# A hybrid encoder layer: the attention's softmax divided after the product with V, x added after the attention's share of the output product, and the state space model's complex tables by three real products

## The chip, the cores and the metric

One core of one Trainium2 chip runs the whole layer in one launch. The metric is the device time in microseconds (us) of that execution; smaller is better. Five engines work side by side, each with a queue of its own: TensorE (PE: products and transposes), VectorE (DVE), ScalarE (ACT), GpSimd (POOL) and SyncE (SP), which here issues all transfers.

## The reference

One layer, x of shape (1, 2048, 1024), float32, cut to what matters:

```python
h = rms_norm(x, norm1); z = h @ w_in                  # q (8 heads x 64) | k, v (2 heads x 64) | u (512)
q, k = rms_norm(q, q_gain), rms_norm(k, k_gain)       # over each head's 64
scores = q k^T / 8 - slope * dist                     # a band: own block of 128 and both neighbours
m = max(max(scores), sink); p = exp(scores - m)
denom = sum(p) + exp(sink - m)
att = (p / denom) @ v                                 # (2048, 512)
# state space model, 32 groups of 16 channels, 64 complex states, both directions:
#   x_t = a x_{t-1} + B u_t  (complex), y = sum of Re(C x) + d u;  then gelu and a gated product
ssm = gelu(y) @ w_glu, value * sigmoid(gate)          # (2048, 512)
x = x + concat([att, ssm]) @ w_out
h = rms_norm(x, norm2)
x = x + square(relu(h @ w_ff1)) @ w_ff2               # d_ff 4096
```

## The kernel before

The sequence is 16 tiles of 128 tokens. A product in full precision is three TensorE products of split operands (`mm3`, lines 87 to 89: high by high, low by high, high by low). The two products of the feed-forward part use a recursion of seven products in place of eight for a 2 by 2 block matrix (`PRODUCTS` 1 to 7), so their operands are sums and differences of blocks.

The stages, in order of time in the profile:

- 0 to 134 us: norm of x, and the u columns of W_in.
- 134 to 345 us: for each tile q, k and v (`qkv_part`, tiles pq and pk), then the norm of q and k over each head: squares on ScalarE, `L924` sums them to ten numbers per token, `L925` to `L932` make their inverse root with one step of Newton, and `L935`, `L939`, `L941` apply it. Beside it runs a side stream with the state space model, in 16 pairs of groups: `pair_in` and `pair_out` build tables by complex products (L564, 512 columns each; six on VectorE for each of the two), and scans (L672, L675) and products (pvu, py, pkd) follow.
- 345 to 690 us: attention, in 32 units (tile n, key head g), each with four query heads. `front(u)` makes scores, maximum and exponentials, `back(u - LEAD)` transposes the probabilities (ptp, copied by ScalarE into pT), multiplies by V (pv) and by the attention's rows of W_out (poa), and adds x (`L1100`). x is loaded here and the sum is stored to x1_dr. The rest of the side stream runs between, at a rate set by `SIDE_STEPS`.
- 690 to 907 us: the gated product (`run_glu`, four quarters) and `out_quarter`: for each tile `out_ssm` makes the state space model's share of W_out (pos_), adds it to x1 read back from x1_dr (two buffers, `L1199`, `L1211`) and stores it; `norm2` follows, with the inverse root on GpSimd (`L1237`), and for each pair of tiles the four sums of blocks on GpSimd (`L1249` to `L1252`). All seven operands of a pair go to hc_dr. The first 1024 tokens' operands are read back (`L1282`) and transposed (pth, `L1292`) as right operands hb.
- 907 to 1540 us: the first feed-forward product (f_al and others), the first 1024 tokens, then the second; 1553 to 2199 us: the second feed-forward product.

A scheduler sets each engine's order within what the program's dependences allow; each engine takes its own queue in order, and a waiting instruction holds up all that stands behind it on that engine. The division in `softmax` before, on the probabilities:

```python
DVE.tensor_tensor(den, den, es, op=ALU.add)
DVE.reciprocal(rc, den)
for h in range(GQ):
    if h < 2: DVE.tensor_scalar(p[:, h, 0:w], p[:, h, 0:w], rc[:, h:h + 1], None, op0=ALU.mult)
    else:     ACT.activation(out=p[:, h, 0:w], in_=p[:, h, 0:w], func=AF.Copy, scale=rc[:, h:h + 1])
```

Of the kernel before, what the change touches and what calls it, by code (L numbers as in the profile page):

```python
# [20 lines left out]
P = 128  # L21
# [24 lines left out]
LEAD = 3  # L46
# [5 lines left out]
SIDE_STEPS = 8 * 61.0 + 16.0  # L52
# [5 lines left out]
def hymba_kernel(ctx: ExitStack, tc: tile.TileContext, x, norm1, w_in, q_gain, k_gain, sink,  # L58
# [9 lines left out]

    ident = cst.tile([P, P], F32, name="ident")
    make_identity(nc, ident)  # L70
    mhalf = cst.tile([P, 16], F32, name="mhalf")
    nc.gpsimd.memset(mhalf, -0.5)

    ACT, DVE, POOL = nc.scalar, nc.vector, nc.gpsimd
    dist = cst.tile([P, 3 * P], F32, name="dist")
    nsink = cst.tile([P, NH], F32, name="nsink")
# [36 lines left out]
    v_all = att.tile([P, NT, NKV * HD], F32, name="v_all")  # L113

# [10 lines left out]
    pv_n = sc.tile([P, NG, C16], F32, name="pv_n")  # L125
    ta_c = sc.tile([P, NG, 8], F32, name="ta_c")
# [3 lines left out]
    rmag = sc.tile([P, NG], F32, name="rmag")  # L130
    dmask = sc.tile([P, GH], F32, name="dmask")
    dcol = sc.tile([64, NG // 2], F32, name="dcol")
# [267 lines left out]
    g1 = pw.tile([P, KD], F32, name="g1")  # L400
# [138 lines left out]
    f_tiles = [{nm: pm.tile([P, 2, 2, GH], F32, name=f"{nm}{j}") for nm in ("f_r", "f_i")} for j in range(2)]  # L539
    yr_t = pm.tile([P, 4 * NCH], F32, name="yr")  # L540
# [61 lines left out]

    def pair_in(i, h):
# [6 lines left out]
        sh = [P, 2, C16, GH]  # L610
        xr, xi = (four(a[:, gs], 2).to_broadcast(sh) for a in (bb_r, bb_i))
        yr, yn = (four(a[:, gs], 3).to_broadcast(sh) for a in (pv_r, pv_n))
        tmp = pm.tile([P, 512], F32, tag="tmp", name="tmp").rearrange("p (g s h) -> p g s h", g=2, s=C16)
        v = {}
        for j, (nm, x1, x2, op) in enumerate((("b_r", xr, xi, ADD), ("b_i", xi, xr, SUB))):
            t = pm.tile(sh, F32, tag=f"v{j}", name="v")
            dv(t, x1, yr, MUL)
            yield
            dv(tmp, x2, yn, MUL)
            yield  # L620
            dv(t, t, tmp, op)
            yield
# [7 lines left out]
            v[nm] = vt  # L630
        yield
# [48 lines left out]
    def ssm_unrotate(i):  # L680
        b = st[i]
        tcs, tsn = b["t_c"], b["t_s"]
        xr, xi = (pm.tile([P, 4 * NCH], F32, tag=nm, name=nm) for nm in ("x_r", "x_i"))
# [15 lines left out]
    def pair_out(i, h):  # L699
# [10 lines left out]
        sh = [P, 2, C16, GH]  # L710
        cr, cn = (four(a[:, gs], 2).to_broadcast(sh) for a in (c_r, c_n))
        er, ei = (four(a[:, gs], 3).to_broadcast(sh) for a in (pw_r, pw_i))
        tmp = pm.tile([P, 512], F32, tag="tmp", name="tmp").rearrange("p (g s h) -> p g s h", g=2, s=C16)
        for nm, x1, x2, op in (("q_r", cr, cn, ADD), ("q_n", cn, cr, SUB)):
            t = pm.tile(sh, F32, tag=nm, name=nm)
            dv(t, x1, er, MUL)
            yield
            dv(tmp, x2, ei, MUL)
            yield
            dv(t, t, tmp, op)  # L720
            b[nm] = t
            yield
# [9 lines left out]
        ks = pm.tile([64, GH + C16 * GH], F32, tag="ks", name="ks")  # L732
# [154 lines left out]
    with tc.tile_pool(name="p1", bufs=2) as p1:  # L887
# [16 lines left out]
        def qkv_part(t):  # L904
# [18 lines left out]
            t3 = p1.tile([P, 10], F32, tag="t3", name="t3")  # L923
# [4 lines left out]
            DVE.tensor_tensor(t3, rs, rs, op=ALU.mult)  # L928
            DVE.tensor_tensor(t3, t3, ms, op=ALU.mult)
# [652 lines left out]
```

## Time and profile before

| | |
|---|---|
| median of 3 runs | 2199.15 us (2194.41 to 2200.61) |
| the profiled execution | 2200.2 us, its span 2198.4 us |
| TensorE busy | 2077.8 us, 95% of the span |
| VectorE, ScalarE, GpSimd busy | 1479.6, 1016.0, 590.3 us |
| mean granted TensorE clock | 0.98 |

The profile's times are of one execution, and busy shares are means over stages with different limits. Ends of matmuls are modelled, so TensorE looks busy through waits that are shorter than a matmul's tail. A line of a group gives the engine's line and operation, what it writes and reads, its count, busy time in us, the mean of one in ns, and the engine's idle time just before with what ended it.

### The profile page before, as it was taken

The page shows a single profiled execution, that of the slowest core. Times are in us where ns is not written, and L with a number is a line of the kernel's source. Part 1 is how long each engine was busy: PE and PEld are TensorE (multiplying, and loading weights), DVE is VectorE, ACT ScalarE, POOL GpSimd, SP SyncE. Part 2 cuts the span into 40 slices and gives each one's busy share as a digit, 9 for nine tenths or more (in the row PEclk, how much of TensorE's full clock was granted, in tenths as well). Part 3 has the DMA queues.
Part 4 walks back from the last instruction along what each step waited for, and adds up shares of the span by engine and source line. Part 5 has one row for each costly group of instructions (what it writes and reads, how often), then busy time and mean ns, then how long its engine had stood idle before and what let it go on. Part 6 is the DMA issues. An engine that isn't in the chain of part 4 may idle for free.

```text
span 2198.4 us, 30479 instructions
## 1 busy us (share of the span) xinstructions
PE 2077.8 (95%) x10546; PEld 1706.7 (78%) x10546; DVE 1479.6 (67%) x2806; ACT 1016.0 (46%) x2061; POOL 590.3 (27%) x451
## 2 busy tenths in 40 slices
PE   7999998999999997799999999999599999999999
PEld 7888886777767786688888788888487778778787
DVE  7959887998856644655445655554677776776765
ACT  4433336767666422455555655555342332333231
POOL 2000000000012223322332133221553663564441
PEclk9999999999999999799999999999799999999999
DMA  8925544333245448644445644442763443443344
GB/s 252 292 82 159 157 125 142 108 100 117 96 125 160 163 153 279 224 149 152 153 158 176 203 156 146 146 151 99 255 212 101 129 128 98 134 130 114 112 135 162
DMA packets 284394, 337.06 MB, mean 153 GB/s; under 512 B 62928, under 2 KB 211408, under 8 KB 284240
## 3 DMA queue, kind: packets, MB, share of 16 engines
q1 hardware_dynamic: 284240, 335.12, 46.9%
q8 instruction: 83, 1.36, 0.3%
q14 instruction: 71, 0.58, 0.1%
HBM read 206.11 MB, written 128.94 MB: 152 GB/s over the span
## 4 chain that ended last, share of the span: by engine, by line
PE 67%; DVE 13%; DMA 7%; POOL 5%; issue 3%; ACT 3%; SPq 1%; DVEq 0%; POOLq 0%; ACTq 0%
PE f L87 6%; PE f L89 6%; PE f L88 6%; PE f_al L89 5%; PE f_al L87 5%; PE f_al L88 5%; PE f_ga L87 3%; PE f_ga L89 3%; PE f_ga L88 3%; POOL w2s L1470 2%; PE pv L1075 1%; POOL fs L1496 1%; PE ptp L1065 1%; DVE acc L1541 1%; PE f_be L89 1%
## 5 line engine op out<-in xcount | busy, mean ns | idle before, releaser
L1541 DVE TENSOR_TENSOR acc<-f,acc 128x512 f32<-128x512 f32 x448 | 304.8, 687 | 164.6 <-PE f L89 158.0
L87 PE MATMUL f<-w2s,fs 128*128 128x512 f32 x896 | 352.9, 394 | 31.0 <-DVE acc L1541 15.7
L89 PE MATMUL f<-w2s,fs 128*128 128x512 f32 x896 | 351.4, 392 | 3.7 <-POOL fs L1496 3.7
L88 PE MATMUL f<-w2s,fs 128*128 128x512 f32 x896 | 351.3, 392 | 0.0
L1495 ACT ACTIVATE fs<-fr 128x512 fp32r<-128x512 f32 x224 | 141.6, 633 | 366.1 <-PE f L89 350.5
L1496 POOL TENSOR_TENSOR fs<-fr,fs 128x512 fp32r<-128x512 f32 x128 | 185.2, 1449 | 297.0 <-ACT fs L1495 255.8
L87 PEld LDWEIGHTS f<-w2s,fs 128*128 128x128 f32 x896 | 169.4, 189 | 74.1 <-ACT fs L1495 27.0
L1339 POOL TENSOR_TENSOR w1s<-w1r,w1s 128x512 fp32r<-128x512 f32 x96 | 135.2, 1409 | 311.9 <-ACT w1s L1338 303.0
L87 PE MATMUL f_al<-hb,w1s 128*128 128x512 f32 x512 | 201.0, 393 | 1.0 <-ACT w1s L1338 1.0
L89 PE MATMUL f_al<-hb,w1s 128*128 128x512 f32 x512 | 200.6, 392 | 1.1 <-DVE w1s L1339 0.9
L89 PEld LDWEIGHTS f<-w2s,fs 128*128 128x128 f32 x896 | 169.7, 189 | 40.3 <-POOL fs L1496 4.5
L88 PE MATMUL f_al<-hb,w1s 128*128 128x512 f32 x512 | 200.4, 391 | 0.0
L88 PEld LDWEIGHTS f<-w2s,fs 128*128 128x128 f32 x896 | 169.8, 190 | 34.7
L818 POOL TENSOR_TENSOR wgl<-wgr,wgh 128x512 fp32r<-128x512 f32 x8 | 10.4, 1311 | 521.0 <-DMA wgr<-in_w_glu_dram 508.2
L1339 DVE TENSOR_TENSOR w1s<-w1c,w1s 128x512 fp32r<-128x512 f32 x96 | 68.3, 711 | 88.0 <-ACT w1s L1338 88.0
L89 PEld LDWEIGHTS f_al<-hb,w1s 128*128 128x128 f32 x512 | 96.5, 189 | 22.0 <-DVE w1s L1339 1.3
L87 PEld LDWEIGHTS f_al<-hb,w1s 128*128 128x128 f32 x512 | 96.5, 189 | 21.3 <-ACT w1s L1338 1.4
L88 PEld LDWEIGHTS f_al<-hb,w1s 128*128 128x128 f32 x512 | 96.6, 189 | 19.6
L1338 ACT ACTIVATE w1s<-w1c 128x512 fp32r<-128x512 f32 x128 | 80.6, 630 | 49.7 <-PE f_al L89 48.4
L88 PE MATMUL f_ga<-hb,w1s 128*128 128x512 f32 x256 | 99.9, 390 | 0.0
L87 PE MATMUL f_ga<-hb,w1s 128*128 128x512 f32 x256 | 99.8, 390 | 0.0
L89 PE MATMUL f_ga<-hb,w1s 128*128 128x512 f32 x256 | 99.7, 389 | 0.0
(548 smaller groups left out, 4956.9 us busy)
## 6 DMA issues: line engine op xcount, KB each, us to landing
fr<-f_dr SPq DMA_DIRECT2D x224, 256.0 KB
w1r<-in_w_ff_dram SPq DMA_DIRECT2D x64, 512.0 KB
f_dr<-fs SPq DMA_DIRECT2D x128, 256.0 KB
f_dr<-f SPq DMA_DIRECT2D x96, 256.0 KB
w2r<-in_w_ff_dram SPq DMA_DIRECT2D x32, 512.0 KB
hs<-hc_dr SPq DMA_DIRECT2D x56, 256.0 KB
xt<-in_x_dram SPq DMA_DIRECT2D x16, 512.0 KB
q_dr<-qd SPq DMA_DIRECT2D x16, 512.0 KB
```

The source lines that it names most:

```text
L87: nc.tensor.matmul(ps_ap, lhsT=lh, rhs=rh, start=first, stop=False, skip_group_check=onto)
L88: nc.tensor.matmul(ps_ap, lhsT=lh, rhs=rl, start=False, stop=False, skip_group_check=onto)
L89: nc.tensor.matmul(ps_ap, lhsT=ll, rhs=rh, start=False, stop=last, skip_group_check=onto)
L818: eng_lo.tensor_tensor(lo, raw, hi, op=ALU.subtract)
L1065: nc.tensor.transpose(pt[:, h, :], p[:, h, kt * P:(kt + 1) * P], ident)
L1075: nc.tensor.matmul(po[g * HD:(g + 1) * HD, :], lhsT=v_all[:, lo + kt, g * HD:(g + 1) * HD], rhs=pT.pop((n, g, kt)), start=kt == 0, stop=kt ...
L1338: ACT.activation(out=t[:, 0], in_=src, func=AF.Copy)
L1339: (DVE if m in (6, 7, 3) else POOL).tensor_tensor(t[:, 1], src, t[:, 0], op=SUB)
L1470: (DVE if m in (6, 7, 3) and fp else POOL).tensor_tensor(t[:, 1], src, t[:, 0], op=SUB)
L1495: ACT.activation(out=t[:, 0], in_=src, func=AF.Copy)
L1496: (DVE if m in (6, 7, 3) else POOL).tensor_tensor(t[:, 1], src, t[:, 0], op=SUB)
L1541: DVE.tensor_tensor(a[:, cs], po, a[:, cs], op=ADD)
```

## The change

It does six things.

1. The probabilities are no longer divided. The eight inverse sums of a tile are spread to 64 columns each (`spread`, ScalarE), transposed by TensorE into a PSUM bank of tag "tr" (`spread_t`), and multiply the product with V (`an`); that product is copied out of PSUM first.
2. x is not added in the attention: the attention's share of W_out goes to x1_dr in halves by way of a ScalarE copy (`xa`). Where x1 is read back, `load_xa` loads x too (one buffer, xx) and adds it, 1024 columns on VectorE.
3. The tables of `pair_in` and `pair_out` come from three real products in place of four (`three`): five VectorE operations of 512 columns in place of six, for `pair_in` a small sum too. Five sums of 512 columns are added to the setup.
4. The inverse root of the q and k norm is a power on GpSimd, and k is scaled once, not in two halves.
5. The second 1024 tokens' operands are transposed straight from SBUF between the out tiles, and FF1 takes that half first. Only the first half goes by way of hc_dr, read back later. Of the last pair, operands 1, 2, 6 and 5 are transposed ahead of FF1 and the others inside its first block.
6. `LEAD` is 2 in place of 3, tiles of few columns are padded, the square's unused output in `norm2` goes to PSUM (tag "mm", two buffers, which pos_ uses too), and the GpSimd subtractions of FF1's first block move to VectorE.

```diff
-LEAD = 3
+LEAD = 2
-SIDE_STEPS = 8 * 61.0 + 16.0
+SIDE_STEPS = 8 * 57.0 + 16.0
...
+    def three(names, tags, name, x1, x2, gs, y1, dif, total, both=None):
+        sh = [P, 2, C16, GH]
+        if both is None:
+            xs = pm.tile([P, 2, GH], F32, tag="xs", name="xs", bufs=2)
+            dv(xs, x1[:, gs], x2[:, gs], ADD)
+        else:
+            xs = both[:, gs]
...
+        dv(tmp, four(xs, 2).to_broadcast(sh), four(y1[:, gs], 3).to_broadcast(sh), MUL)
+        yield None, None
+        for nm, tag, x, y, op in ((names[0], tags[0], x2, dif, ADD), (names[1], tags[1], x1, total, SUB)):
+            t = pm.tile(sh, F32, tag=tag, name=name)
+            dv(t, four(x[:, gs], 2).to_broadcast(sh), four(y[:, gs], 3).to_broadcast(sh), MUL)
+            yield None, None
+            dv(t, tmp, t, op)
+            yield nm, t
...
             DVE.tensor_reduce(ms, sq, axis=AX.X, op=ALU.add)
-            DVE.tensor_scalar(ms, ms, 1.0 / HD, EPS, op0=ALU.mult, op1=ALU.add)
-            ACT.activation(out=rs, in_=ms, func=AF.Sqrt)
-            DVE.reciprocal(rs, rs)
...
-            DVE.tensor_tensor(rs, rs, t3, op=ALU.mult)
+            DVE.scalar_tensor_tensor(ms, ms, HD * EPS, hsc, op0=ALU.add, op1=ALU.mult)
+            POOL.tensor_tensor(rs, ms, mhalf[:, 0:10], op=ALU.pow)
...
+        def spread_t(n):
+            pr_ = ps.tile([P, GQ, P], F32, tag="tr", name="ptr")
             for h in range(GQ):
+                nc.tensor.transpose(pr_[:, h, :], rb_t[n][:, h].rearrange("p g d -> p (g d)"), ident)
+            rT_t[n] = pr_
...
-            ACT.activation(out=ah, in_=pa3, func=AF.Copy)
-            DVE.tensor_tensor(al, pa3, ah, op=ALU.subtract)
+            ACT.copy(an, po.rearrange("p (h t) -> p h t", h=GQ))
+            DVE.tensor_tensor(an, an, rT_t.pop(n), op=ALU.mult)
+            ACT.activation(out=ah, in_=an, func=AF.Copy)
+            DVE.tensor_tensor(al, an, ah, op=ALU.subtract)
...
-            DVE.tensor_tensor(xr[:, cs], po, xr[:, cs], op=ALU.add)
-            if half == 1:
-                nc.sync.dma_start(out=x1_dr[n * P:(n + 1) * P, :], in_=xr)
+            xa = pb.tile([P, 512], F32, tag="xa", name="xa", bufs=2)
+            ACT.copy(xa, po)
+            nc.sync.dma_start(out=x1_dr[n * P:(n + 1) * P, cs], in_=xa)
...
+    def load_xa(n, bufs):
+        t = load_x1(n, po_, "x1", bufs)
+        xt = po_.tile([P, D], F32, tag="xx", name="xx", bufs=1)
+        nc.sync.dma_start(out=xt, in_=x2d[n * P:(n + 1) * P, :])
+        DVE.tensor_tensor(t, t, xt, op=ALU.add)
+        return t
...
-    early = right_operands(0, [(m, i) for i in range(4) for m in PRODUCTS])
-    for n, _ in enumerate(out_quarter(3)):
-        if n > 0:
-            for _ in range(7):
-                next(early, None)
+    x1 = load_xa(NT // 2, 2)
+    pend = None
+    for n in range(NT // 2, NT):
+        nx = load_xa(n + 1, 2) if n + 1 < NT else None
+        out_ssm(n, x1)
+        if n == 11:
+            sb_stack.close()
+        nc.sync.dma_start(out=x1_dr[n * P:(n + 1) * P, :], in_=x1)
+        if pend is not None:
+            for m in PRODUCTS:
+                trans(m, (n - NT // 2) // 2 - 1, pend[m])
+        if n == NT - 1:
+            for j, m in enumerate((1, 2)):
+                trans(m, 3, h2_t[n - 1][:, j * 512:j * 512 + 512])
+        pend = norm2(n, x1)
+        x1 = nx
```

Three places show how the instructions stand. VectorE in the qkv stage, one tile's norm of q and k (msq and rsq are its sums and inverse roots, the lines of 512 columns between belong to the side stream); before:

```order
L924 TENSOR_REDUCE msq<-sq 128x10
L564 TENSOR_TENSOR tmp<-bb_r,pv_n 128x512
L925 TENSOR_SCALAR msq<-msq 128x10
L564 TENSOR_TENSOR v<-v,tmp 128x512
L927 RECIPROCAL rsq<-rsq 128x10
L564 TENSOR_TENSOR tmp<-c_n,pw_i 128x512
L928 TENSOR_TENSOR t_2805<-rsq 128x10
L929 TENSOR_TENSOR t_2805<-t_2805,msq 128x10
L931 TENSOR_TENSOR rsq<-rsq,hsc 128x10
L930 TENSOR_SCALAR t_2805<-t_2805 128x10
L932 TENSOR_TENSOR rsq<-rsq,t_2805 128x10
L935 TENSOR_TENSOR sq<-pq,rsq 128x512
```

and of the change:

```order
L942 TENSOR_REDUCE msq<-sq 128x10
L578 TENSOR_TENSOR b_i<-b_i,t_c 128x512
L943 SCALAR_TENSOR_TENSOR msq<-msq,hsc 128x10
L947 TENSOR_TENSOR sq<-pq,rsq 128x512
L950 TENSOR_TENSOR kd<-pk,rsq 128x256
L954 TENSOR_TENSOR qd<-sq,qd 128x8x64
```

Of the short operations L925 to L932 one is left (L943), and L947, which needs the power that GpSimd makes of L943's output, stands right behind it here. In six of the 16 tiles nothing stands between the two, in the other ten one instruction.

VectorE in the output product, tiles 12 and 13 (before x_9115 is tile 12, x_9117 tile 13; in the change x_8913 and x_8965; ss and h belong to `norm2`); before:

```order
L1211 TENSOR_TENSOR x_9115<-pos__9119,x_9115 128x512
L1211 TENSOR_TENSOR x_9115<-pos__9133,x_9115 128x512
L1235 TENSOR_TENSOR ss_9149<-ss_9149 128x1
L1236 TENSOR_SCALAR ss_9149<-ss_9149 128x1
L1238 SCALAR_TENSOR_TENSOR h_9148<-x_9115,ss_9149,g_7874 128x1024
L1211 TENSOR_TENSOR x_9117<-pos__9160,x_9117 128x512
L1211 TENSOR_TENSOR x_9117<-pos__9174,x_9117 128x512
```

and of the change:

```order
L1253 TENSOR_TENSOR x_8913<-pos__8970,x_8913 128x512
L1293 TENSOR_TENSOR t_8958<-h_8948 128x512
L1253 TENSOR_TENSOR x_8913<-pos__8984,x_8913 128x512
L1241 TENSOR_TENSOR x_8965<-x_8965,xx 128x1024
L1342 TENSOR_TENSOR hb<-pth,hb 128x4x128 x2
L1278 TENSOR_TENSOR ss_9049<-ss_9049 128x1
L1279 TENSOR_SCALAR ss_9049<-ss_9049 128x1
L1281 SCALAR_TENSOR_TENSOR h_9048<-x_8913,ss_9049,g_8711 128x1024
L1342 TENSOR_TENSOR hb<-pth,hb 128x4x128 x2
L1253 TENSOR_TENSOR x_8965<-pos__9063,x_8965 128x512
```

The sum of the next tile's x1 and x (L1241, x_8965) now stands between a tile's out sums and its norm. The load of x1 for the tile after that waits, by its two buffers, for the norm (h_9048) behind it.

TensorE at the end of the output product (pth<-ident,h and pth<-ident,t are the transposes from SBUF; h_9192 is tile 14's norm, h_9245 tile 15's, the t's sums of the last pair); before:

```order
L88 MATMUL pos__9407<-wsl,sth 128x512
L89 MATMUL pos__9407<-wsh,stl 128x512
L1292 MATMUL pth<-ident,hs 128x128 x72
L87 MATMUL f_al<-hb,w1s 128x512
```

and of the change:

```order
L93 MATMUL pos__9216<-wsl,sth 128x512
L94 MATMUL pos__9216<-wsh,stl 128x512
L1340 MATMUL pth<-ident,h_9192 128x128 x8
L1340 MATMUL pth<-ident,t_9256 128x128 x4
L1340 MATMUL pth<-ident,h_9245 128x128 x4
L92 MATMUL f_al<-hb,w1s 128x512
```

Where 72 transposes of operands read back stood ahead of FF1, 16 stand now, eight of which need the last tile's norm and GpSimd's sums of it.

## Rows read from the trace of the kernel before

In a row of a group: busy us, mean ns of one, then idle time just before it and what ended most of it.

**Rows 1.** Busy time by stretch (its first line names the columns).
```profile
core 0: us, PE busy (x) PEld busy (x) DVE busy (x) ACT busy (x) POOL busy (x), PEclk, DMA share, GB/s
134.00:345.00 211.00, 199.97 (x1348) 173.31 (x1346) 191.32 (x436) 71.45 (x198) 1.11 (x11) 0.99 0.45 136
345.00:384.00 39.00, 28.33 (x179) 21.93 (x179) 28.49 (x98) 30.63 (x82) 0.00 (x0) 0.91 0.56 162
384.00:630.00 246.00, 241.08 (x1539) 184.83 (x1538) 211.46 (x579) 173.13 (x462) 0.00 (x0) 1.00 0.33 104
...
850.00:907.00 57.00, 37.58 (x182) 28.80 (x181) 28.12 (x47) 21.56 (x43) 12.99 (x13) 0.80 0.90 298
```

**Rows 2.** Groups of VectorE by line, 134 to 345 us.
```profile
L939 DVE TENSOR_TENSOR kd<-pk,rsq 128x128 f32<-128x128 f32 x30 | 7.2, 279 | 0.0
...
L564 DVE TENSOR_TENSOR v<-bb_r,pv_r 128x512 f32<-128x512 f32 x10 | 6.8, 684 | 17.2 <-DMA u_dr<-ut 17.2
...
L927 DVE RECIPROCAL rsq<-rsq 128x10 f32<-128x10 f32 x15 | 3.1, 209 | 1.8 <-ACT rsq L926 1.8
...
L932 DVE TENSOR_TENSOR rsq<-rsq,t 128x10 f32<-128x10 f32 x15 | 2.5, 166 | 0.3
```

**Rows 3.** TensorE in order of time, 230 to 243 us (start, length, instruction).
```profile
234.91 1.05 PE L637 MATMUL pvu<-u,vt 128*128 128x128 f32 x8
...
239.28 0.40 PE L89 MATMUL pq<-wqh,hl 128*128 128x512 f32 x1
239.52 0.40 PE L87 MATMUL pq<-wqh,hh 128*128 128x512 f32 x1
```

**Rows 4.** Groups of VectorE by line, 345 to 690 us.
```profile
L1054 DVE TENSOR_SCALAR p<-p,rc 128x384 f32<-128x384 f32 (+1 forms) x64 | 24.0, 416 | 0.4
L1100 DVE TENSOR_TENSOR xr<-poa,xr 128x512 f32<-128x512 f32 x32 | 21.8, 687 | 5.7 <-PE poa L89 4.1 <-DMA xr<-in_x_dram 1.4
L1082 DVE TENSOR_TENSOR al<-pv,ah 128x512 fp32r<-128x512 f32 x16 | 10.9, 680 | 3.1 <-ACT ah L1081 3.1
```

**Rows 5.** Groups of ScalarE by line, 345 to 690 us.
```profile
L1067 ACT COPY pT<-ptp 128x512 f32<-128x512 f32 x92 | 50.8, 582 | 21.0 <-PE ptp L1065 20.7
L1056 ACT ACTIVATE p<-p,rc 128x384 f32<-128x384 f32 (+1 forms) x64 | 35.1, 596 | 8.2 <-DVE rc L1051 7.8 <-DVE ks L736 0.2
```

**Rows 6.** SyncE's queue in order of time, 774 to 800 us.
```profile
776.95 0.32 SPq L1261 DMA_DIRECT2D x_dr<-x  x1
...
781.06 0.39 SPq L1199 DMA_DIRECT2D x<-x_dr  x1
...
791.68 0.37 SPq L1199 DMA_DIRECT2D x<-x_dr  x1
```

**Rows 7.** VectorE in order of time, 864 to 912 us.
```profile
877.57 0.69 DVE L1211 TENSOR_TENSOR x<-pos__9393,x 128x512 f32<-128x512 f32 x1 [3.67 <-DMA x<-x_dr]
...
881.02 1.28 DVE L1238 SCALAR_TENSOR_TENSOR h<-x,ss,g 128x1024 f32<-128x1024 f32 x1 [0.73 <-POOL ss L1237]
...
908.77 1.77 DVE L1339 TENSOR_TENSOR w1s<-w1c,w1s 128x512 fp32r<-128x512 f32 x1
```

**Rows 8.** TensorE in order of time, 864 to 912 us.
```profile
872.62 0.40 PE L89 MATMUL pos__9407<-wsh,stl 128*128 128x512 f32 x1
879.71 1.94 PE L1292 MATMUL pth<-ident,hs 128*128 128x128 f32 x8 [6.69 <-DMA hs<-hc_dr]
...
906.99 0.79 PE L87 MATMUL f_al<-hb,w1s 128*128 128x512 f32 x1 [1.03 <-ACT w1s L1338]
```

**Rows 9.** SyncE's queue in order of time, 826 to 909 us.
```profile
871.07 0.94 SPq L1199 DMA_DIRECT2D x<-x_dr  x1
...
900.70 2.07 SPq L1322 DMA_DIRECT2D w1r<-in_w_ff_dram  x4
```

**Rows 10.** Groups of VectorE by line, 690 to 907 us.
```profile
L1238 DVE SCALAR_TENSOR_TENSOR h<-x,ss,g 128x1024 f32<-128x1024 f32 x16 | 20.5, 1284 | 12.8 <-POOL ss L1237 12.1 <-DMA x<-x_dr 0.7
```

**Rows 11.** GpSimd in order of time, 784 to 800 us.
```profile
785.82 1.29 POOL L1249 TENSOR_TENSOR t<-h 128x512 f32<-128x512 f32 x1 [1.40 <-DVE h L1238]
```

More of the change, by code (lines that the diff above doesn't have):

```diff
@@ L399, in hymba_kernel @@
     wql = pw.tile([P, KD, 768], F32R, name="wql")
-    g1 = pw.tile([P, KD], F32, name="g1")
+    g1 = small(pw, KD, name="g1")
     hstack = ExitStack()
@@ L709, in pair_out @@
             b[nm] = f
[L710 to L721, printed above, removed]
+        for nm, t in three(("q_r", "q_n"), ("q_r", "q_n"), "q", c_r, c_n, gs, pw_r, pw_d, pw_s, c_s):
+            if t is not None:
+                b[nm] = t
             yield
@@ L1137, in back @@
             n, g = divmod(u, 2)
+            if g == 1 and n < NT:
+                sums(n)
             if n < NT:
@@ L1140, in back @@
                     p_trans(n, g, kt)
+                    if g == 1 and kt == 0:
+                        spread(n)
                     yield 0.44
@@ L1245, in norm2 @@
         t4 = pn.tile([P, 512], F32, tag="t4", name="t4")
-        nc.sync.dma_start(out=hc_dr[n // 2, 1], in_=b11)
-        nc.sync.dma_start(out=hc_dr[n // 2, 2], in_=b21)
-        nc.sync.dma_start(out=hc_dr[n // 2, 3], in_=b22)
-        POOL.tensor_tensor(t3, b22, b12, op=SUB)
+        first = n < NT // 2
+        if first:
+            for m, t in ((1, b11), (2, b21), (3, b22)):
+                nc.sync.dma_start(out=hc_dr[n // 2, m], in_=t)
+        (POOL if first else DVE).tensor_tensor(t3, b22, b12, op=SUB)
         POOL.tensor_tensor(b12, b12, b11, op=SUB)
@@ L1408, in hymba_kernel @@
     load_w1(1)
+    left_w1(0, (1, 2))
+    for m in (1, 2):
+        split_w1(0, m)
     left_w1(0)
[L1410 removed]
+    for m in PRODUCTS[2:]:
         split_w1(0, m)
@@ L1415, in hymba_kernel @@
         blk = ff1_block(g)
-        switch = right_operands(1, [(m, i) for m in PRODUCTS for i in range(4)]) if g == NFB - 1 else None
+        switch = right_operands(0, [(m, i) for m in PRODUCTS for i in range(4)]) if g == NFB - 1 else None
         def after(m, g=g, switch=switch):
@@ L1425, in hymba_kernel @@
         next(blk)
+        if g == 0:
+            next(blk)
         if g + 1 < NG1:
@@ L1433, in hymba_kernel @@
             load_w1(g + 2)
-        for _ in range(5):
-            after(next(blk))
+        if g == 0:
+            after(2)
+            for m in PRODUCTS[2:6]:
+                trans(m, 3, pend[m])
+                after(next(blk))
+            trans(4, 3, pend[4])
+            pnb_stack.close()
+            ph_ = d1_stack.enter_context(tc.tile_pool(name="ph_", bufs=1))
+        else:
+            for _ in range(5):
+                after(next(blk))
         last = (blk, after)
```

169 lines of the change are left out of this document (89 added, 80 removed).

## The prediction

> **What bounds the kernel now.** I read the busy time by stretch first, then the groups of the busiest engine in each, then the order of time where TensorE stands still. TensorE is busy 95% of the whole, so a gain has to come from a stretch where something else sets its pace, and the change touches only what lies between 134 and 907 us. Of the rest, the two feed-forward products keep nearly all their code.
>
> 134 to 345 us is VectorE's: 191.3 of 211 us busy, and 17.2 of its idle time is a single wait at the start, for u [rows 1, 2]. After that it hardly stops. TensorE shows 200.0 us, but its ends are modelled: one matmul of 512 columns lasts 0.40 us in the rows and the next starts 0.24 us after it [rows 3]. Priced by distance, 16 tiles x 24 x 0.24 = 92 us for q, the same number at half the columns 46 us for k and v, and the remaining 580 of the 1348 matmuls at about 0.11 (eight of them in 1.05 us with one tail of 0.28) 64 us: some 200 us of work at most, 185 if the 0.24 is partly waiting. So TensorE stands right behind VectorE, with 11 to 26 us between.
>
> 345 to 384 us is the filling of the attention's pipeline: TensorE 28.3 of 39. From 384 to 630 us it is at 241.1 of 246 with VectorE at 211.5: here TensorE is the bound and VectorE follows [rows 1]. From 850 to 907 TensorE is busy 37.6 of 57 us and its granted clock is 0.80, while the transfers are at 0.90 [rows 1]. The last out product starts at 872.6, FF1 at 907.0: 34.4 us in which TensorE only transposes operands read back from DRAM and waits for them, once 6.7 us [rows 8].
>
> **The change, stretch by stretch.**
>
> *qkv, 134 to 345 us.* Removed per tile: seven short VectorE operations of 0.17 to 0.21 us, one added: net 6 x 0.17 = 1.0 us, 16 us in all; the k scaling, two of 0.28 us to one that I put at 0.45, 2 us [rows 2]. Of the 32 tables 18 fall in this stretch (10 and 8 of the two kinds, as the counts stand); each loses one operation of 0.68 us, less ten small sums at 0.2: 10 us. Together 28 us off VectorE. Added: L947 waits for GpSimd's power. Where a VectorE operation in `norm2` waits for such a power, it idles 0.73 us [rows 7]; in six tiles nothing covers that and in ten one instruction does, so 6 x 0.8 + 10 x 0.15 = 6 us. VectorE would save 22, and TensorE's own work allows 11 to 26, of which some stays waiting for hand-overs. I take -12, bounds -20 and -4. The five sums of the setup (3.4 us) fall in the 17.2 us wait for u; uncovered they would cost just that.
>
> *Attention, 345 to 690 us.* VectorE loses 24.0 (the division) and 21.8 (adding x), gains 16 multiplies at 0.68 = 11 us, loses about 14 x 0.68 = 10 us of tables and some 8 us of short operations whose number is halved: -53 of 274. ScalarE loses 64 x 0.596 = 38 us and gains 64 copies of 512 columns at 0.58 = 37: nothing [rows 4, 5]. But TensorE, the bound, gains 64 transposes at 0.11 us, +7, and saves no matmul. What it can get back is waiting: 10.7 us in the filling, 4.9 in the middle [rows 1], and what the modelled ends hide. One unit of `LEAD` less shortens the filling; I put 6 us there and 9 us for hand-overs that a freer VectorE makes sooner: -15 + 7 = -8. Bounds: -20 if all waits shown and the hidden ones go, +7 if none do. The new chain from spread over transpose, multiply and subtract lies two units behind the scores; a "tr" bank held for it would cost TensorE's next transposes up to 1 us a tile, and that is in the upper bound.
>
> *Output product, 690 to 907 us.* Removed: the gap of 34.4 us, of which the 72 transposes are 72 x 0.11 = 8 us of work that only moves, so 26 us of standing still. Three terms come back.
>
> First, the end. After the sum of x1 and x of tile 15, VectorE still has, in order, tile 14's norm, tile 15's out sums and tile 15's norm, then GpSimd two block sums. By the rows a norm takes 3.4 us from its last out sum to its end (two out sums of 0.69 from 877.57 end at about 878.9, the h behind them ends at 882.3), hence 3.5 + 0.7 x 5 (two out sums, three copies of operands) + 3.5, then 2 x 1.29 on GpSimd [rows 7, 11] and 1 us for transpose and copy: 14 us. TensorE's last out product runs into the first 3 of them and transposes fill about 1: +10.
>
> Second, the loop. x1 of tile n+1 may be loaded once the norm of tile n-1 is done, and that norm now stands behind the sum of x1 and x of tile n. One turn is: copies and norm 3.5 us, the load, the sum of x1 and x. The load: 871.07 to 877.57, 6.5 us, in a stretch of crowded transfers [rows 7, 9]; 781.06 was issued 4.1 us after the store of tile 0 that it waits for, so a quieter transfer takes about 4.1, and I take 4.6 [rows 6]. The sum: 1.28, as the norm's operation of 1024 columns with two operands from SBUF, which is the nearest row [rows 10]. In all 9.4 us, where TensorE needs 24 x 0.24 + 14 x 0.11 = 7.3. Four of the five turns from tile 10 to 15 are such loops, one is short: 4 x 9.4 + 5 = 43 against 37 us, +6.
>
> Third, the first eight tiles. There each fourth load of a quarter already stands in SyncE's queue behind the hc_dr stores that wait for GpSimd (781.06 the third, 791.68 the fourth [rows 6]), and xx and its sum now stand behind it: 2.5 us a quarter, 5, less about 3 for the third quarter, whose hc_dr stores are gone: +2.
>
> Sum: -26 + 10 + 6 + 2 = -8. Bounds: -22 if loads come in 4 us and the loop hides, +14 if every load takes 6.5.
>
> A rule that speaks against this: VectorE's subtraction at 908.77, two operands from SBUF while GpSimd ran one of its own, took 1.77 us where 0.69 is usual [rows 7]. The Trainium skill, SBUF - State Buffer, "Who interferes with whom", says that a VectorE instruction with two SBUF inputs contends with a GpSimd instruction that reads SBUF. By it the sums of x1 and x would stretch where they meet the block sums, and the whole would come some 5 us later than I forecast; no row shows such a sum yet.
>
> *FF1 and after.* Code as before but for the first block, where three operands of the last pair are transposed between products and their sums run on VectorE: +1, bounds -2 and +6.
>
> **Sum**: -12 - 8 - 8 + 1 = -27 against the profiled execution's 2200.2 us (1 us above the median): 2173.
>
> **The rivals.**
>
> *The loop in every tile (slower).* If the sum of x1 and x holds up VectorE's queue in both halves, with loads of 6.5 us and more under 1.5 MB a tile, ten tiles (two in each of the first two quarters, six in the second half) turn at 12 us in place of 7: +50, less 16 that the end still saves, +34; with -12, -8 and +1 the whole is +15, 2215. It decides from 3.5 us a tile on, that is a turn of 10.5 us. For it speaks the 3.67 us that VectorE waited for x at 877.57; against it that the 28 stores and 28 loads of operands that crowded the transfers there are gone. 0.14.
>
> *TensorE was the bound (no change).* VectorE's 75 us are freed where TensorE had little to gain: -4 in qkv, +7 in attention, -8 and +1: 2196. For it 241.1 of 246 us; against it the 11 to 26 us in qkv. 0.16.
>
> *Everything comes through.* -20, -18, -18, 0: 2144. For it, that VectorE's saving is three times what I book. 0.17.
>
> My forecast has 0.53.
>
> **How the numbers follow.** The range reaches from just above the full gain to the rival of no change: 2148 to 2202, which leaves out most of the slow rival and half of the full gain, about 0.2. A measurement tells 0.3% (6.6 us) from no change. Faster by more: 0.45 of my case, 0.17, and 0.06 of the no-change rival: 0.68. Within: 0.06 and 0.08, and 0.01 of the slow one: 0.15. Slower: 0.02, 0.02 and 0.13: 0.17.
>
> **What would show it.** Right: the qkv stretch about 12 us shorter, VectorE there below 170 us; in the attention VectorE near 220 us and TensorE's share unchanged; turns of the x1 sums of 9 to 10 us in tiles 12 to 15; FF1 starting near 879. Wrong: qkv as long as before with TensorE at 95% of it (TensorE was the bound); waits of TensorE for "tr" banks in the attention; sums of x1 and x of 2 us and more beside GpSimd; VectorE waiting over 5 us for x1 in each tile.

## The result and the profile after

The changed kernel takes 2234.72 us (median of 4 runs, 2229.36 to 2239.9) where the kernel before, run beside it, takes 2199.8: a ratio of 1.0164, 95% interval 1.0133 to 1.0195. It is slower by 35 us, where I had forecast 27 us less; the measured time lies outside the range of 2148 to 2202.

The profiled execution has a span of 2235.3 us. To place the 37 us I measure three stages in both traces by the starts of TensorE's products in order of time: qkv from the first pq to the last pk, attention from there to the last poa, output from there to the first f_al.

| stage | before | after | difference | forecast |
|---|---|---|---|---|
| qkv | 211.1 | 228.0 | +16.9 | -12 |
| attention | 335.6 | 366.4 | +30.8 | -8 |
| output | 226.6 | 214.9 | -11.7 | -8 |
| FF1 (f_al) | 630.3 | 631.3 | +1.0 | +1 |

Of the attention's 30.8 us 5.7 are moved work: 42 products of the gated part (pglu) stand in it after and 20 before, at 0.26 us each, and they are gone from the output stage. So without moved work the output stage is 6 us better and the attention 25 worse. After FF1 nothing differs by more than a microsecond.

Busy time by stretch of the changed kernel, the columns as in [rows 1]; 134 to 362 us is its qkv stage, and 402 to 680 us does what 384 to 630 us does there (some 100 scores, 75 copies of transposed probabilities):

```profile
134.00:362.00 228.00, 205.68 (x1366) 177.34 (x1365) 174.88 (x331) 68.71 (x187) 34.55 (x26) 0.98 0.44 126
...
402.00:680.00 278.00, 263.61 (x1625) 192.38 (x1626) 176.78 (x465) 175.12 (x451) 0.00 (x0) 0.99 0.23 73
...
887.00:943.00 56.00, 42.71 (x210) 34.26 (x207) 38.35 (x57) 19.39 (x43) 17.39 (x16) 0.89 0.43 149
```

VectorE is busy 174.9 us in a stage that grew to 228, against 191.3 of 211 [rows 1]; in the steady attention 176.8 of 278 against 211.5 of 246. VectorE has less to do, and the stages are longer with it. The engine that shrank is not the one that set the end.

In the qkv stage VectorE's groups by line show the new wait (busy time and mean ns of one, then the idle time before them and what ended it):

```profile
L947 DVE TENSOR_TENSOR sq<-pq,rsq 128x512 f32<-128x512 f32 x15 | 10.4, 692 | 29.2 <-POOL rsq L944 29.2
...
L950 DVE TENSOR_TENSOR kd<-pk,rsq 128x256 f32<-128x256 f32 x15 | 6.2, 414 | 0.0
```

and GpSimd's, in the same view of the same stage, what it waits for:

```profile
L944 POOL TENSOR_TENSOR rsq<-msq,mhalf 128x10 f32<-128x10 f32 x15 | 33.4, 2229 | 179.8 <-DVE msq L943 172.0 <-DVE xs L578 7.8
```

The power of ten columns takes GpSimd 2.23 us, and VectorE stands still for it 29.2 us in 15 tiles, 1.95 each. The wait from which I priced it, 0.73 us [rows 7], was for a power of one column, which takes 0.55 us (the kernel before):

```profile
880.43 0.55 POOL L1237 TENSOR_TENSOR ss<-ss,mhalf 128x1 f32<-128x1 f32 x1 [13.55 <-DVE ss L1236]
```

The merged k scaling takes 0.41 us, near the 0.45 I put.

So TensorE's waits in the stage (those that the profile shows, of all kinds) grew from 11.0 to 22.1 us; the largest single line, for whom, with us in total, times and the longest, is that for tt, a table that goes out to DRAM (ks) and comes back. Before and after:

```profile
PE py L759 <- DMA tt<-kd_dr: 4.5, 5, 2.4
```

```profile
PE py L777 <- DMA tt<-kd_dr: 7.4, 4, 3.2
```

In the attention TensorE's waits name the new chain; before, neither of these two lines was there:

```profile
PE poa L92 <- ACT ah L1110: 6.9, 7, 1.4
...
PE ptp L1090 <- DVE an L1109: 4.7, 5, 1.5
```

The product with W_out waits for ah, which now comes after a copy and a multiply; and the transposes of the probabilities wait for the multiply that frees the bank of tag "tr".

In the output stage the end is as forecast. In its last stretch above, 887 to 943, TensorE has 42.7 of 56 us at a granted clock of 0.89, against 37.6 of 57 at 0.80 in [rows 1]. TensorE in order of time, to compare with [rows 8]:

```profile
932.48 0.39 PE L94 MATMUL pos__9216<-wsh,stl 128*128 128x512 f32 x1
932.71 1.03 PE L1340 MATMUL pth<-ident,h 128*128 128x128 f32 x8
941.06 1.12 PE L1340 MATMUL pth<-ident,t 128*128 128x128 f32 x4 [7.32 <-POOL t L1295]
...
943.38 0.80 PE L92 MATMUL f_al<-hb,w1s 128*128 128x512 f32 x1 [0.35 <-ACT w1s L1400]
```

From the last out product to FF1 are 10.9 us in place of 34.4. The wait is for GpSimd's sum (t, L1295), as the order had it. The sums of x1 and x on VectorE, in order of time:

```profile
896.27 1.22 DVE L1241 TENSOR_TENSOR x<-x,xx 128x1024 f32<-128x1024 f32 x1
...
904.68 1.48 DVE L1241 TENSOR_TENSOR x<-x,xx 128x1024 f32<-128x1024 f32 x1 [1.75 <-issue]
...
915.31 1.22 DVE L1241 TENSOR_TENSOR x<-x,xx 128x1024 f32<-128x1024 f32 x1
...
922.83 1.49 DVE L1241 TENSOR_TENSOR x<-x,xx 128x1024 f32<-128x1024 f32 x1 [0.90 <-DMA x<-x_dr]
```

They turn in 8.4, 10.6 and 7.5 us, where I put 9.4. The load of x1 is issued right behind the norm, as the loop had it, and the sum follows a load of about 3.5 us in the first and the last of the three turns; in the second other instructions of VectorE, waits for ScalarE and the out sums among them, stand ahead of the sum when the load has had its 3.5 us, so that the load does not set that turn. SyncE's issue for the first turn (the norm's h ends at 901.13):

```profile
901.20 0.32 SPq L1233 DMA_DIRECT2D x<-x_dr  x1
```

One more row answers to the rule weighed in the prediction. Of the 16 sums of x1 and x five ran beside GpSimd's block sums. The other eleven took 1.21 to 1.23 us; four of the five took 1.48, 1.49, 2.14 and 2.33, the longest here with the two block sums beside it:

```profile
856.42 2.33 DVE L1241 TENSOR_TENSOR x<-x,xx 128x1024 f32<-128x1024 f32 x1
```

```profile
855.65 2.01 POOL L1295 TENSOR_TENSOR t<-h 128x512 f32<-128x512 f32 x1
857.74 2.15 POOL L1296 TENSOR_TENSOR t<-h,t 128x512 f32<-128x512 f32 x1
```

The fifth, at 785.72, took 1.22, and there the block sum took 2.20 in place of 1.29. That agrees with the Trainium skill, SBUF — State Buffer, "Who interferes with whom" (two operands from SBUF beside a GpSimd instruction that reads SBUF). The four together are 2.5 us longer, half of the 5 that the prediction weighed.

### The profile page after: what moved, and what is told of

Its sections match the earlier page's. It is cut to its first block, busy times and chain, and to the rows that moved or that the text cites. A ratio compares the mean times of both kernels' runs of the same rounds, so it can differ in the third digit from the quotient of the medians.

```text
span 2235.3 us, 30317 instructions
## 1 busy us (share of the span) xinstructions
PE 2098.6 (94%) x10610; PEld 1713.4 (77%) x10610; DVE 1444.0 (65%) x2579; ACT 1009.0 (45%) x2027; POOL 618.7 (28%) x459
## 4 chain that ended last, share of the span: by engine, by line
PE 44%; DVE 5%; POOL 3%; issue 2%; DMA 2%; ACT 0%; SPq 0%; DVEq 0%; POOLq 0%; ACTq 0%
PE f L92 6%; PE f L94 6%; PE f L93 6%; PE f_al L92 5%; PE f_al L94 5%; PE f_al L93 5%; PE f_ga L93 2%; PE f_ga L94 2%; PE f_ga L92 2%; POOL w2s L1546 2%; POOL fs L1572 1%; DVE acc L1617 1%; PE f_be L94 1%; PE f_be L93 1%; PE f_be L92 1%
## 5 line engine op out<-in xcount | busy, mean ns | idle before, releaser
L1401 POOL TENSOR_TENSOR w1s<-w1r,w1s 128x512 fp32r<-128x512 f32 x93 | 129.9, 1397 | 300.6 <-ACT w1s L1400 292.8
L1047 DVE CUSTOM_DVE_ANT_0 p<-pss,dist 128x384 f32<-128x384 f32 (+1 forms) x128 | 66.6, 537 | 65.8 <-PE pss L1046 62.0
L836 POOL TENSOR_TENSOR wgl<-wgr,wgh 128x512 fp32r<-128x512 f32 x8 | 10.6, 1341 | 330.6 <-DMA wgr<-in_w_glu_dram 321.5
L93 PE MATMUL f_ga<-hb,w1s 128*128 128x512 f32 x256 | 100.1, 391 | 1.4 <-DVE hb L1342 1.4
L92 PE MATMUL f_ga<-hb,w1s 128*128 128x512 f32 x256 | 99.9, 390 | 0.0
```

Source lines behind the costliest of these rows:

```text
L92: nc.tensor.matmul(ps_ap, lhsT=lh, rhs=rh, start=first, stop=False, skip_group_check=onto)
L93: nc.tensor.matmul(ps_ap, lhsT=lh, rhs=rl, start=False, stop=False, skip_group_check=onto)
L836: eng_lo.tensor_tensor(lo, raw, hi, op=ALU.subtract)
L1047: DVE.tensor_tensor_reduce(out=p_t[n, g][:, h, 0:w], in0=pss, in1=dist[:, off:off + w], scale=-SLOPE[g * GQ + h], scalar=-3.0e38, op0=ALU. ...
L1401: (DVE if m in (6, 7, 3) or g == 0 else POOL).tensor_tensor(t[:, 1], src, t[:, 0], op=SUB)
```

## The experiments

The theories: **A**, the GpSimd power and the division after the product each cost by themselves; **B**, both stages are longer because `LEAD` is 2 and the side stream is paced anew. Later ones are named where they come. Stage times are read as in the table above; ratios are to the kernel before on the same chip. A stage time is that of one profiled execution, which lies up to 7 us from its kernel's median (2201.8 against 2194.6 in "before, less VectorE"). Kernels with the same code in a stage show how far such times can be trusted: 225.8 to 228.0 us for qkv in the four with the power, 366.4 and 368.5, and 348.7 and 350.0, for the attention in two pairs. A difference of some 2 us is therefore read as none.

| kernel | median us | ratio (95%) | qkv | attention | output |
|---|---|---|---|---|---|
| changed | 2234.7 | 1.0164 (1.0133, 1.0195) | 228.0 | 366.4 | 214.9 |
| norm undone | 2228.8 | 1.0141 (1.0051, 1.0232) | 221.1 | 368.5 | 215.5 |
| division undone | 2215.1 | 1.0085 (1.0051, 1.0119) | 225.8 | 348.7 | 216.4 |
| both undone | 2207.3 | 1.0049 (1.0032, 1.0067) | 220.0 | 350.0 | 213.3 |
| both, py later | 2203.8 | 1.0043 (1.0027, 1.0060) | 213.6 | 349.0 | 212.9 |
| both and tables undone | 2203.8 | 1.0024 (1.0011, 1.0037) | 212.9 | 349.0 | 219.7 |
| and LEAD 3 | 2187.7 | 0.9954 (0.9936, 0.9972) | 214.7 | 338.3 | 214.1 |
| and x in the attention | 2187.4 | 0.9952 (0.9930, 0.9974) | 212.2 | 338.8 | 211.3 |
| and py later | 2193.2 | 0.9992 (0.9981, 1.0003) | 212.6 | 344.8 | 211.2 |
| tables undone, LEAD 3 | 2208.4 | 1.0056 (1.0030, 1.0081) | 222.3 | 346.2 | 212.5 |
| before, LEAD 2 | 2203.6 | 1.0024 (1.0008, 1.0041) | 212.0 | 341.6 | 227.4 |
| before, less VectorE | 2194.6 | 0.9987 (0.9976, 0.9998) | 210.0 | 337.2 | 228.7 |
| before, more VectorE | 2208.2 | 1.0039 (1.0022, 1.0056) | 212.5 | 343.4 | 225.8 |
| chain, no transposes | 2221.1 | 1.0128 (1.0093, 1.0162) | 226.0 | 358.9 | 209.1 |
| transposes, no chain | 2215.2 | 1.0089 (1.0054, 1.0124) | 227.4 | 348.8 | 215.1 |

**The norm's power undone**, to the changed kernel:

```diff
-            DVE.scalar_tensor_tensor(ms, ms, HD * EPS, hsc, op0=ALU.add, op1=ALU.mult)
-            POOL.tensor_tensor(rs, ms, mhalf[:, 0:10], op=ALU.pow)
+            DVE.tensor_scalar(ms, ms, 1.0 / HD, EPS, op0=ALU.mult, op1=ALU.add)
+            ACT.activation(out=rs, in_=ms, func=AF.Sqrt)
...
+            DVE.tensor_tensor(rs, rs, t3, op=ALU.mult)
```

> The changed kernel with the q and k norm's inverse root made as before (seven short VectorE operations and ScalarE's square root in place of the GpSimd power); all else as changed. Theory A (the power of ten columns takes GpSimd 2.2 us, VectorE stands still behind it 29 us in the qkv stage): the qkv stage, from its first pq to its last pk product, falls from 228 to 203 to 212 us, the attention stays at 360 to 370, the whole is 2209 to 2220. Theory B (both stages are longer because the side stream is paced differently and LEAD is 2): the qkv stage stays at 222 us or more, the whole within 6 us of 2235.

The qkv stage falls by 6.9 us to 221.1, between the two theories: the power costs, but of VectorE's 29 us of standing still only 7 reach the end of the stage, and 10 of the 17 us have another cause. With the division undone in both kernels the same step is 5.8 us (225.8 to 220.0). The attention doesn't move. The whole can't tell, since the kernel's two runs lie 14 us apart. In this kernel TensorE's largest wait of the stage has grown:

```profile
PE py L777 <- DMA tt<-kd_dr: 13.1, 5, 3.4
```

py, in TensorE's order, waits for the table, here longer than in either kernel above.

**The division undone**, to the changed kernel: each head's probabilities are multiplied by its inverse sum in `softmax`, and `pv` splits the product from PSUM.

```diff
-            ACT.copy(an, po.rearrange("p (h t) -> p h t", h=GQ))
-            DVE.tensor_tensor(an, an, rT_t.pop(n), op=ALU.mult)
-            ACT.activation(out=ah, in_=an, func=AF.Copy)
-            DVE.tensor_tensor(al, an, ah, op=ALU.subtract)
+            ACT.activation(out=ah, in_=pa3, func=AF.Copy)
+            DVE.tensor_tensor(al, pa3, ah, op=ALU.subtract)
```

> The changed kernel with the probabilities divided before they are transposed, as before (no spread, no ptr transposes, no multiply of the product with V); LEAD 2, the tables and x added later stay. Theory A (the transposes of the spread sums and the chain copy, multiply, split, subtract behind the product with V hold up TensorE): the attention, from the last pk to the last poa product, falls from 366 to 335 to 348 us, the whole is 2204 to 2218. Theory B (LEAD 2 and the pacing): the attention stays at 358 us or more.

The attention falls by 17.7 us to 348.7, the whole to 2215.1: near what theory A said, though VectorE is busier in the stage by 13 us (229.6 to 242.4) and ScalarE by 13 (239.3 to 251.9).

**Both undone.**

> Both of the above undone in the changed kernel: the tables by three products, x added later, the second half's operands from SBUF and LEAD 2 stay. Theory A: the two losses add, 2180 to 2197 us, under the kernel before. Theory B: over 2215.

2207.3: the two losses add, or nearly (by the medians 6.0 and 19.6 alone, 27.5 together; by the ratios 0.23%, 0.79% and 1.15%), but what is left is still slower than before, 0.49%, by 220.0 against 211.1 in qkv and 350.0 against 335.6 in the attention. Neither theory was enough. Theory **C** came from the wait for tt above: the tables by three products lengthen a round trip for which TensorE waits.

**LEAD 2 alone**, to the kernel before:

```diff
-LEAD = 3
+LEAD = 2
...
-                if h % 2 and u > 1 and wo_parts:
+                if h and u > 1 and wo_parts:
```

> The kernel before with LEAD 2 in place of 3 alone (and the split of W_out one call earlier, as the change has it, which LEAD 2 needs). Theory A: the attention is 330 to 342 us and the whole within 6 us of before. Theory B: the attention is 350 us or more, the whole 2212 or more.

6.0 us in the attention, of which eight more pglu products are 2, and +0.24% in the whole: a cost, where I had booked a gain of 6 us for a shorter filling. The filling is shorter: the first poa product starts 35.3 us after the last pk product, where it was 39.3. But what follows is 10 us longer, and TensorE's waits that the profile shows don't tell why (16.3 us in the stage, 20.2 before). It is far from the whole of theory B.

**The tables undone too**, to the kernel with both undone: `three` is out, `pair_in` and `pair_out` are as before.

> As the kernel with norm and division undone, and the tables by four products again (six VectorE operations of 512 columns for two tables in place of five, the side stream's rate as before). Theory C: in the qkv stage TensorE waits for the round trip of kd through DRAM (ks stored, tt loaded), which fewer steps between a table and its product no longer cover; then the qkv stage falls from 220 to 209 to 214 us, the attention from 350 to 337 to 345, the whole is 2186 to 2198. Theory D (the padded tiles, the merged k scaling or the x1 copies are what holds both stages): the qkv stage stays at 217 us or more.

The qkv stage falls by 7.1 us to 212.9, the attention stays at 349.0. So theory C holds for qkv and fails for the attention, and theory D, which has the stage at 217 us or more, is out. The whole gains 3.5 us by the medians and 0.25% by the ratios, whose intervals overlap, since the output stage gives 6.4 back (11 pglu products, 2.9 us of it, moved from the attention); the rest of that I can't place. The power stays in both the changed kernel and "tables undone, LEAD 3", and there the tables make 5.7 us in qkv (228.0 to 222.3).

**The later product**, which tests the round trip by itself: tables by three products stay, and py of a group's first pair is issued after the next group's first table.

```diff
-            yield from pair_y(i, 0)
             if i + 1 < NB4:
                 yield from pair_in(i + 1, 0)
+            yield from pair_y(i, 0)
             yield from pair_out(i, 1)
```

> The kernel with norm and division undone (tables by three products, LEAD 2), and in the side stream the product py of a group's first pair is issued after the next group's first table instead of before it, eight steps more between the store of ks and the product that needs tt. Theory C (TensorE waits in its order for the round trip of kd, 11.7 us in six waits, and loses its clock behind the long ones): those waits fall below 5 us, the qkv stage from 220 to 209 to 215 us, the whole to 2194 to 2203. Theory F (the table's own order is what slows the stage, not the trip): the qkv stage stays at 217 us or more.

TensorE's waits for tt in the two kernels, without and with the move:

```profile
PE py L777 <- DMA tt<-kd_dr: 11.7, 6, 2.7
```

```profile
PE py L777 <- DMA tt<-kd_dr: 2.6, 2, 2.0
```

The waits for tt fall from 11.7 to 2.6 us and the stage from 220.0 to 213.6, as theory C said and theory F did not: where py stands in TensorE's order matters. The whole can't confirm it: 6.4 us are 0.3%, the ratio falls by 0.06%, and each interval is 0.17% to either side. Nor is it the waits' length alone. With the move another wait comes in, for VectorE's table ahead of its transposes:

```profile
PE ptv L652 <- DVE v L578: 6.0, 4, 2.3
```

In all TensorE's waits in the stage fall by only 3 us (14.2 to 11.3). The rest of the 6.4 us is near what the clock gives back: the stage's mean granted clock, in the column before the last two, is 0.97 without the move and 0.99 with it, which over 214 us is some 4 us of full clock (an estimate from these figures).

```profile
134.00:354.00 220.00, 205.75 (x1365) 178.78 (x1363) 184.77 (x422) 73.61 (x203) 1.11 (x11) 0.97 0.45 130
```

```profile
134.00:348.00 214.00, 202.23 (x1364) 174.50 (x1362) 182.06 (x420) 73.94 (x205) 1.11 (x11) 0.99 0.47 134
```

In the stretch after the longest of the waits for tt, without and with the move:

```profile
174.00:182.00 8.00, 7.38 (x35) 6.93 (x36) 6.18 (x16) 1.10 (x2) 0.00 (x0) 0.58 0.13 46
```

```profile
174.00:182.00 8.00, 6.72 (x55) 6.31 (x55) 8.00 (x21) 2.36 (x6) 0.00 (x0) 1.00 0.60 172
```

TensorE ran 35 matmuls at a mean granted clock of 0.58 there (mostly the lower level, 1.2 GHz), where with the wait gone it ran 55, not all of them the same ones, at 1.00.

**LEAD 3, and x added in the attention again**, each on top of the one before:

> The same with LEAD 3: what is left of the change is x added later, the k scaling in one, the padded tiles and the second half's operands from SBUF. If LEAD 2 costs what it did alone (6 us in the attention), the attention is 331 to 339 us, the output stage 211 to 217 and the whole 2180 to 2191, faster than before. If LEAD 2 costs nothing here, the whole is within 3 us of the kernel above.

> The same with x added in the attention as before, so that of the change little but the second half's operands from SBUF is left. If the sum of x1 and x costs in the output stage what the loop in the prediction says (6 to 10 us) and the ScalarE copies bring nothing to the attention, the output stage is 203 to 210 us and the whole 2174 to 2186. If taking the sum off VectorE pays in the attention, the attention is 4 us longer or more than in the kernel above and the whole is not faster.

LEAD 3 takes 10.7 us off the attention (9 without seven pglu products that move), as expected if LEAD 2 costs, and both kernels are faster than the one before: 2187.7 and 2187.4, ratios of 0.9954 and 0.9952, with intervals clear of 1. Where x is added makes no difference in the whole: taking 32 sums of 512 columns off VectorE in the attention is worth nothing there that could be told (338.3 against 338.8), and the loop in the output stage costs 2.8 us, 4 without the five pglu products that move, less than the 6 to 10 expected. What is left of the change in the faster one, the second half's operands from SBUF, takes 15.3 us off the output stage (211.3 against 226.6). The padded tiles, the one k scaling and the side stream's x_r and x_i, which now lie in other tiles' buffers, a change that the list of six leaves out, stay in this kernel too, and its qkv stage is near the kernel before's (212.2 against 211.1).

**The move on top of that:**

> The same move in the kernel that keeps of the change the second half's operands from SBUF, the k scaling and the padding, with tables by four products, LEAD 3 and x added in the attention. TensorE's waits for tt are 8 us or less there already, so Theory C gives 2 to 6 us in the qkv stage (206 to 211 us) and 2180 to 2187 for the whole; if VectorE is the bound of that stage instead, nothing (within 2 us of 2187).

Nothing in qkv (212.2 to 212.6), and 6 us lost in the attention: a miss. The waits for tt fell here too, from 5.3 to 1.7 us, but a wait for the table (ptv, 5.9 us) took their place as above, and the stage's clock, 0.99 without the move already, had nothing to give back. In the attention's first 40 us TensorE's clock is lower with the move (0.74 against 0.87), and one wait of 6.5 us for ScalarE's copy stands in it:

```profile
PE ptq L1024 <- ACT pT L1094: 6.5, 1, 6.5
```

**The division at LEAD 3**, the changed kernel with the tables undone:

```diff
-LEAD = 2
+LEAD = 3
...
-            xa = pb.tile([P, 512], F32, tag="xa", name="xa", bufs=2)
+            xa = pb.tile([P, 512], F32, tag="xa", name="xa", bufs=1)
```

> The changed kernel with the tables by four products and LEAD 3 (one buffer for xa in place of two, for space): the division after the product and the GpSimd power stay. Theory A (the chain behind the product with V and the transposes cost by themselves): the attention is 350 us or more, the whole 2206 to 2222. Theory E (they cost only since LEAD 2 leaves no slack): the attention is 342 us or less.

346.2 us, between theory A and theory E: against 338.3 with the division on the probabilities it costs 7.9 us here, against 17.7 at LEAD 2. So part of its price seems to be the slack that LEAD 2 took away; the two pairs differ in the tables, the norm and xa's buffers too, so that this is not shown alone.

**Which half of the division costs.** Both kernels leave the division itself out. In the first the product is multiplied by a constant tile and nothing is transposed; in the second copy and multiply are gone and the bank is read by one column only:

```diff
-                if kt == hi - lo - 1:
-                    spread_t(n)
...
-            DVE.tensor_tensor(an, an, rT_t.pop(n), op=ALU.mult)
+            DVE.tensor_tensor(an, an, woh.bitcast(F32)[:, :, 0:P], op=ALU.mult)
```

```diff
-            ACT.copy(an, po.rearrange("p (h t) -> p h t", h=GQ))
-            DVE.tensor_tensor(an, an, rT_t.pop(n), op=ALU.mult)
-            ACT.activation(out=ah, in_=an, func=AF.Copy)
+            DVE.tensor_scalar(nm_t[n][:, 0:1], rT_t.pop(n)[:, 0, 0:1], 1.0, None, op0=ALU.mult)
+            ACT.activation(out=ah, in_=pa3, func=AF.Copy)
```

> The changed kernel without the transposes of the spread sums: the product with V is multiplied by a constant tile from SBUF instead (the sums' copy on ScalarE stays; the division itself is left out). If TensorE's 64 transposes and the tr bank that they hold are the loss, the attention falls from 366 to 347 to 353 us, the whole to 2214 to 2222. If the chain copy, multiply, split, subtract behind the product with V is, it stays at 358 us or more.

> The changed kernel with the transposes kept (one column of each bank is read, which frees it) and the product with V split straight from PSUM as before, without copy and multiply (the division is left out). If the chain is the loss, the attention falls to 350 to 357 us; if the transposes and the bank are, it stays at 360 us or more.

Without copy and multiply the attention is 348.8 us, where the division undone had 348.7, with the 64 transposes still there; of the 17.6 us that it falls, eight pglu products that move are 2. Without the transposes it is 358.9, and TensorE's wait behind the chain is the larger for it:

```profile
PE poa L92 <- ACT ah L1108: 15.3, 8, 3.2
```

So it is the chain. The transposes cost 7.5 us beside it, and some 2 without it (nine pglu products fewer stand in the 348.8 us than in the 348.7). That this is because the bank is held until the chain's multiply has read it fits the 4.7 us of ptp behind an above, but no run shows it alone.

**VectorE's share of the bound in qkv**, which the prediction began with: the kernel before without the step of Newton, and with two of them.

```diff
             DVE.tensor_tensor(t3, rs, rs, op=ALU.mult)
             DVE.tensor_tensor(t3, t3, ms, op=ALU.mult)
             DVE.tensor_scalar(t3, t3, -0.5, 1.5, op0=ALU.mult, op1=ALU.add)
+            DVE.tensor_tensor(rs, rs, t3, op=ALU.mult)
+            DVE.tensor_tensor(t3, rs, rs, op=ALU.mult)
+            DVE.tensor_tensor(t3, t3, ms, op=ALU.mult)
+            DVE.tensor_scalar(t3, t3, -0.5, 1.5, op0=ALU.mult, op1=ALU.add)
```

> The kernel before with the step of Newton left out of the q and k norm (the inverse root is ScalarE's alone, so q and k are a little less exact): four short VectorE operations a tile less, 10 us off VectorE in the qkv stage, and no GpSimd power. If VectorE is the bound of the stage, as the prediction has it, the stage falls from 211 to 201 to 206 us and the whole to 2186 to 2191. If TensorE's own work and its waits in its order hold it, the stage stays at 209 us or more and the whole within 3 us of before.

> The kernel before with the step of Newton made twice: four short VectorE operations a tile more, 10 us on VectorE. If VectorE is the bound, the stage grows to 217 to 222 us and the whole to 2201 to 2207. If TensorE holds the stage and VectorE has room, the stage grows by 4 us or less.

The 60 short operations are 10 us by their durations added up, but their records overlap, and VectorE's busy time in the stage changes by half of that: 191.1 us before, 185.7 and 195.8. The stage changes by -1.1 and +1.4 us, no more than the spread above. A larger step says the same: in "both, py later" VectorE is busy 179.2 us in the 211 us of [rows 1], and its stage is 213.6.

```profile
134.00:345.00 211.00, 199.65 (x1339) 172.71 (x1338) 179.18 (x413) 72.42 (x198) 1.11 (x11) 0.99 0.48 135
```

VectorE is not the stage's bound; it fills it, and what counts of it is where TensorE waits for one of its results (ptv behind v above). The kernel with more VectorE work is all the same 0.39% slower in the whole, most of it in the attention's filling, where one wait of 5.8 us stands and the clock is low (busy time of its stretch; 0.91 in [rows 1]):

```profile
346.00:386.00 40.00, 27.19 (x144) 20.99 (x144) 28.74 (x98) 27.21 (x75) 0.00 (x0) 0.74 0.44 143
```

## Why the prediction was wrong

*What bounds qkv.* The step that failed first: "134 to 345 us is VectorE's". 191 of 211 us busy was true and decided nothing: 5 us of busy time off or on move the stage by about one, and with 12 off, by the tables and the move of py, it is no shorter. By the rows TensorE, whose ends are modelled, was the bound with what waits in its order, which I had named as a rival ("TensorE was the bound", 0.16) but with no loss in it; no run takes work off TensorE in that stage, so this half is argued. The 28 us off VectorE were too many as well: I added up durations that overlap, and its busy time fell by 16 (191.1 to 175.0).

*The power.* I added 6 us of VectorE's waiting from a row of one column; it was 29. The term of the sum was mis-sized five times, and it cost 6 to 7 us of the stage, not the difference, since VectorE had room.

*The tables.* Booked as 10 us off VectorE in qkv. They cost 6 to 7 us there, by a wait that I did not consider, TensorE's product behind the round trip of ks and tt through DRAM (4.5 us before, 7.4 in the changed kernel and 11.7 with norm and division undone), and with the lower clock that goes with it. The trip is less covered from both sides: over the seven trips of the stage, tables by three against before, the first load of tt is issued 39.4 us after ks in place of 34.9, and TensorE's own work between the last pkd product and py is 73.5 us in place of 77.0, with nearly the same number of products (44 to 77, before 49 to 77). Why the issue comes later stays open.

*The attention.* I had TensorE as the bound there, and 38 us less of VectorE's busy time (267.8 to 229.6, where I booked 53) shortened nothing. But I booked -15 us of waits got back against +7 for transposes. No wait came back in sum: those that the profile shows went from 20.2 to 25.6 us. The upper bound of +7 is the transposes alone; the "tr" bank, 1 us a tile, is said to be in it and is not, and there is no price for the chain copy, multiply, split, subtract, which lies between two products of TensorE: 15 to 18 us of the 25 at LEAD 2, 8 at LEAD 3. LEAD 2 itself, booked as a gain of 6 us, costs: 6 us alone (4 without moved work), 10.7 with x added later (9). The two losses overlap.

*The output stage.* Right in its first two terms and in the sum: 10.9 us left of the gap of 34.4 where I had 10, turns of 7.5 to 10.6 where I had 9.4, and 6 us less in all (without moved work) where I had 8. The third term, the first eight tiles, was not measured alone. The slow rival, "the loop in every tile", had the right sign for a wrong reason: x1 and x cost 3 to 4 us.

Open: 6 to 8 us in the attention come with edits of other places (the move of py, the second step of Newton). Both kernels have one wait of 6 us in the attention's filling and a mean granted clock of 0.74 in its 40 us, where the kernels beside them have 0.87 and 0.91. What brings the wait and the lower clock was not tested.

## What to carry to other kernels

A busy share of 90% does not by itself make a bound: before an engine's work is cut, add and remove a little of it and see whether the stage follows. Ask of each edit what it puts between two instructions of the engine that does set the pace; two operations there cost 15 to 18 us, while 38 us less busy time on VectorE in the same stage gave nothing that could be seen. A price from one column holds for one column, and durations added up are not busy time.

## What the runs showed of the hardware

The power on GpSimd grows with the columns: 0.55 us for one, 2.23 for ten, so some 0.19 us a column and 0.36 besides (an estimate, a line through the two).

A wait in TensorE's order can cost more than its length. In the kernel with norm and division undone one of 2.7 us, which ended at 174.6, was followed by a mean granted clock of 0.58 from 174 to 182 us; products of 512 columns started 0.43 us apart there, and 0.23 before the wait. Not every wait does: one of 2.3 us in the same kernel, which ended at 229.5, was not (busy time and clock around it):

```profile
226.00:230.00 4.00, 1.68 (x10) 1.17 (x9) 4.00 (x10) 0.21 (x1) 0.00 (x0) 1.00 0.49 134
230.00:234.00 4.00, 3.63 (x33) 3.31 (x31) 3.38 (x11) 0.63 (x1) 0.00 (x0) 1.00 0.28 78
```

A VectorE sum of 1024 columns with both operands from SBUF took 1.21 to 1.23 us alone, and up to 2.33 beside GpSimd's block sums; the block sums beside these took up to 2.20 us, where 1.29 is usual.
